# The sample rows' layer norm: mean from row sums of the weights, squares summed by ScalarE

## The chip, the cores and the metric

The kernel runs on one core of a Trainium2 chip. The metric is the device time of one execution in microseconds (us). Before the change it is 280.36 us, the median of three runs (280.11 to 280.70).

## The reference, cut to what matters

One inference step of a decoder with two layers and 1024 features, for 256 prompt rows and 8 sample rows. Layer 0 is a gated short convolution, layer 1 block-sparse attention. Each ends in a residual layer norm. The change sits in the last one, for the 8 sample rows:

```python
ys = (os_.reshape(Bs, Ts, D_MODEL) * jax.nn.silu(zs)) @ w_out_attn[j]
...
xs = _layernorm(DN_ALPHA * xs + ys, ln_g[i], ln_b[i])
...
def _layernorm(x, g, b):
    mu = x.mean(-1, keepdims=True)
    var = jnp.square(x - mu).mean(-1, keepdims=True)
    return (x - mu) * lax.rsqrt(var + LN_EPS) * g + b
```

## The kernel before, in words

Everything is written for one core in one fixed order; each engine runs its own list, and semaphores tie them. Weights come as slabs of 128x1024 floats, one a slot, over SyncE's queue (`load`, L112). ScalarE rounds a slab to its high part (`hi`, L124), VectorE subtracts for the low part (`lo`, L129), and TensorE multiplies high by high, high by low and low by high. Slots 0 to 31 are layer 0's input projection, 32 to 39 its output projection, 40 to 71 layer 1's input projection with attention between, 72 to 79 the slabs of layer 1's output projection. `begin(n)` issues what is hooked to slot n.

The end of the program, where the change lies, runs so:

- In slots 65 to 67 VectorE transposes x (features on partitions) into `kall` (`turn`, L884), and in slots 68 to 71 sixteen transfers on SyncE's queue, four a slot, move it back into `xf` as rows (`turn_move`, L889). Between them on the same queue stand the loads of the slabs 76 to 79, and behind them those of the gains `gb` and `g8`. The samples are taken out of `xf` beforehand by GpSimd (`sample_x`, L909) and turned by VectorE in slot 68 (`sample_turn`, L912). They lie in one tile `sx`, as 128 partitions of 128 features: the eight samples times eight feature groups, with every value twice in order to fill it. `xst` is x, `gs` the mixer's output (`sample_g`, L807), `so` the result.
- Prompt rows 0 to 127: TensorE forms their output projection `c0` in two banks over the eight slabs (`om`, L961). VectorE adds it to x (`evac`, L925), takes the statistics (`stats`, L928; `spread`, L931 and the Sqrt on ScalarE, L932), and the normalization is shared: columns 0 to 511 on VectorE (`one`, L939, and `two`, L944), 512 to 1023 on ScalarE and GpSimd (`other_way`, L951 to L953).
- Prompt rows 128 to 255 in three pieces of columns: 0 to 511 (in an `acc` bank), 512 to 767 (`c1b`), 768 to 1023 (`c1c`), 24 products each, with evacuation and statistics after each piece.
- The samples: 64 products `so` of the raw slabs with `gs` (L1062), each in two passes at full precision. While TensorE does them, VectorE normalizes rows 128 to 255.
- The samples' norm: VectorE adds x to `so` (L1073), takes statistics of each partition (L1074), spreads them over eight columns (L1076), a product with a 0/1 matrix from `g8` gathers the partitions of one sample (`st`, L1079), VectorE aggregates (L1083), ScalarE takes the root (L1084), and three VectorE operations (L1085 to L1087) finish. `ys_o` is stored (L1088).

Of the kernel before, what the change touches and what calls it, by code (L numbers as in the profile page):

```python
# [10 lines left out]
F32 = mybir.dt.float32  # L11
# [3 lines left out]
AF = mybir.ActivationFunctionType  # L15
ALU = mybir.AluOpType
AX = mybir.AxisListType

D = 1024
T = 256  # L20
B = 8
N = T + B
# [3 lines left out]
ALPHA = math.sqrt(2.0)  # L26
# [23 lines left out]
def build(tc, a):  # L50
    nc = tc.nc
    pe, act, dve, pool, sp = nc.tensor, nc.scalar, nc.vector, nc.gpsimd, nc.sync

    with ExitStack() as top:
# [4 lines left out]
        lnp = top.enter_context(tc.tile_pool(name="lnp", bufs=1))  # L59
        psp = top.enter_context(tc.tile_pool(name="psp", bufs=1, space=bass.MemoryType.PSUM))  # L60

        def acc_full():
            return psp.tile([128, 512], F32, tag="acc", bufs=3, name="acc")
# [4 lines left out]
        def att_tile(nm):  # L68
            return psp.tile([128, 512], F32, tag="att", bufs=3, name=nm)
# [20 lines left out]
        xf = cp.tile([128, NB, N], F32, name="xf")  # L90

        epst = cp.tile([128, 1], F32, name="epst")
# [5 lines left out]
        ident = cst[:, C_ID:C_ID + 128]  # L98
# [5 lines left out]
        raws, his, los = {}, {}, {}  # L104
# [41 lines left out]
        def run(n, phase):  # L146
            for f in hooks.pop((n, phase), []):
                f()
# [21 lines left out]
        def begin(n, end=True):  # L170
            for ph in ("dma", "pe", "s0", "hi", "lo", "s1a", "s1b", "s1", "s1c"):
                run(n, ph)
            if end:
                split_late(n)

        def split_late(n):
            run(n, "hi3")
            run(n, "lo3")
# [57 lines left out]
        onem = cp.tile([128, 2, 32], F32, name="onem")  # L236
# [161 lines left out]
        st = cst[:, C_ST:C_ST + 128].rearrange("p (r f b) -> p r f b", r=2, f=8)  # L398
# [129 lines left out]
        with tc.tile_pool(name="l1", bufs=1) as p1, ExitStack() as late_pool:  # L528
# [326 lines left out]
            for h in range(8):  # L855
                n = S + 16 + h
# [18 lines left out]

            turned = kall[:, 0:2048].rearrange("p (c m q) -> p c m q", c=8, m=8)
            xsb = xst = so = gs = g8 = None
            xt = xf.rearrange("p m n -> p (m n)")[:, 0:2048]

            def kv_tile(nm):  # L880
                return kvp.tile([128, 1024], F32, tag="kv", name=nm)
# [17 lines left out]
            def sample_room():  # L899
                nonlocal xsb, xst, so, gs, g8  # L900
                sx = kv_tile("sx")
                xsb, xst, so = (sx[:, 128 * i:128 * i + 128] for i in range(3))
                gs = sx[:, 512:1024].rearrange("p (c k r) -> p c k r", c=2, r=32)
                g8 = kv_tile("g8")[:, 0:392]
                pool.memset(sx, 0.0)

            def sample_x():
# [2 lines left out]

            def sample_turn():
                dve.transpose(xst, xsb)  # L912

            class Rows:

# [39 lines left out]
            def wide(d, k):  # L955
                return d[72 + k].rearrange("p a b -> p (a b)")

            def om(acc, k, c, c0, c1):
                t = np.s_[128 * c:128 * c + 128]
                for i, (m, d) in enumerate(((0, his), (1, his), (0, los))):  # L960
                    pe.matmul(acc, g[m][:, k, t], wide(d, k)[:, c0:c1],  # L961
                              start=k == 0 and i == 0, stop=k == 7 and i == 2)

            at(S + 26, "s1", sample_room)
            at(S + 26, "s1", sample_x)
            at(S + 28, "s1", sample_turn)
            for m in range(8):
                at(S + 25 + m // 3, "s1", turn, m)
# [15 lines left out]
            ps = ln.bcast_mm()  # L984
# [18 lines left out]
            for i in range(2, 32):  # L1003
                n = S + i
# [27 lines left out]
            ac = [ac[:, 512 * i:512 * i + 512] for i in range(2)]  # L1032
            for k in range(8):
                begin(72 + k)
                for h in range(2):
                    om(ac[h], k, 0, 512 * h, 512 * h + 512)
            r = rows[0]
# [7 lines left out]
            r.other_way(512, 1024)  # L1045
            r.two(0, 512)
            sp.dma_start(a["y_o"][0:128], r.x)

            r = rows[1]
            parts = [(0, 512), (512, 768), (768, 1024)]  # L1050
            last = [acc_full(), att_tile("c1b"), att_tile("c1c")]
            for i, (acc, (c0, c1)) in enumerate(zip(last, parts)):
                for k in range(8):
                    om(acc[:, 0:c1 - c0], k, 1, c0, c1)
                r.evac(c0, c1, acc[:, 0:c1 - c0])
                r.stats(i, c0, c1)

            ps = att_tile("so")[:, 0:128]
            for k in range(8):
                for c in range(2):  # L1060
                    for j in range(4):
                        pe.matmul(ps[32 * j:32 * j + 32], gs[:, c, k, :],  # L1062
                                  wide(raws, k)[:, 256 * j + 128 * c:256 * j + 128 * c + 128],
                                  start=k == 0 and c == 0, stop=k == 7 and c == 1)
            r.spread(3)
            r.one(0, 512)
            r.inverse()
# [1 line left out]
            r.two(0, 512)  # L1069
            sp.dma_start(a["y_o"][128:256, 0:512], r.x[:, 0:512])  # L1070
            r.one(512, 768)
            st = lnp.tile([128, 60], F32, name="row2")
            dve.scalar_tensor_tensor(so, xst, ALPHA, ps, ALU.mult, ALU.add)  # L1073
            dve.bn_stats(st[:, 0:6], so)  # L1074
            own8 = st[:, 12:60].rearrange("p (q e) -> p q e", e=6)
            dve.tensor_tensor(own8, g8[:, 384:392].rearrange("p (q o) -> p q o", o=1).to_broadcast([128, 8, 6]),  # L1076
                              st[:, 0:6].rearrange("p (o e) -> p o e", o=1).to_broadcast([128, 8, 6]), ALU.mult)
            t = att_tile("st")[:, 0:48]
            pe.matmul(t, g8[:, 256:384], st[:, 12:60], start=True, stop=True)  # L1079
            r.two(512, 768)  # L1080
            sp.dma_start(a["y_o"][128:256, 512:1024], r.x[:, 512:1024])

            dve.bn_aggr(st[:, 6:8], t)  # L1083
            act.activation(st[:, 8:9], st[:, 7:8], AF.Sqrt, bias=epst)  # L1084
            dve.scalar_tensor_tensor(so, so, st[:, 6:7], g8[:, 0:128], ALU.subtract, ALU.mult)  # L1085
            dve.reciprocal(st[:, 9:10], st[:, 8:9])
            dve.scalar_tensor_tensor(so, so, st[:, 9:10], g8[:, 128:256], ALU.mult, ALU.add)  # L1087
            sp.dma_start(a["ys_o"], so)  # L1088
# [75 lines left out]
```

## Time and profile before

| | before |
|---|---|
| median of three runs | 280.36 us |
| the profiled execution | 280.45 us |
| its span (first to last record) | 278.7 us |
| TensorE busy | 272.7 us, 98% |
| VectorE busy | 195.6 us, 70% |
| ScalarE busy | 155.3 us, 56% |
| mean granted TensorE clock | 0.996 |

Times in the trace are us from the span's start. A row of a timeline gives start, length, engine, line, operation, and output and input tiles; in square brackets stands how long the engine was idle before it and what ended that. PE is TensorE, DVE VectorE, ACT ScalarE, POOL GpSimd, SPq SyncE's queue. A matmul's shown length overlaps the next one's, so prices of products are taken from start to start.

### The profile page before, as it was taken

How to read it: one execution, taken by the hardware profiler on the slowest of the kernel's cores; microseconds unless marked ns; L12 is line 12 of the kernel's file. 1: busy time of each engine (PE TensorE's matmuls, PEld its weight loads, DVE VectorE, ACT ScalarE, POOL GpSimd, SP SyncE). 2: the span in 40 equal slices, each digit the busy share in tenths (PEclk: the TensorE clock that was granted, in tenths of full speed). 3: DMA queues.
4: the chain of work that ended last, by engine and by line, in shares of the span. 5: the costliest groups of instructions: out<-in, count | busy, mean ns of one | idle time of the engine just before them, and what ended most of it. 6: DMA issues, size and time to landing. Idle time of an engine off the chain costs nothing.

```text
span 278.7 us, 6245 instructions
## 1 busy us (share of the span) xinstructions
PE 272.7 (98%) x2330; PEld 255.6 (92%) x2330; DVE 195.6 (70%) x377; ACT 155.3 (56%) x294; POOL 59.8 (21%) x130
## 2 busy tenths in 40 slices
PE   8999999999999999999999999999999999999992
PEld 5999999999999999999998997999959987988891
DVE  3868976655766768969999498498626384993745
ACT  4876564444655538557776495567746752571101
POOL 2110532020101102850311158411100030000212
PEclk9999999999999999999999999999999999999998
DMA  7985989999666876134025999999864995781012
GB/s 230 410 266 189 310 274 331 385 373 356 230 211 224 295 238 221 43 119 152 2 75 194 387 399 348 359 335 304 277 223 149 311 379 173 236 290 61 0 78 85
DMA packets 24495, 66.34 MB, mean 238 GB/s; under 512 B 3090, under 2 KB 6930, under 8 KB 24466
## 3 DMA queue, kind: packets, MB, share of 16 engines
q1 hardware_dynamic: 24178, 65.63, 67.4%
q8 instruction: 18, 0.29, 0.4%
q10 hardware_dynamic: 288, 0.33, 0.4%
q14 instruction: 11, 0.09, 0.1%
HBM read 61.55 MB, written 3.35 MB: 233 GB/s over the span
## 4 chain that ended last, share of the span: by engine, by line
PE 98%; DVE 1%; issue 0%
PE acc L136 24%; PE acc L138 24%; PE acc L137 24%; PE c L961 4%; PE sd L716 3%; PE dps L768 3%; PE acc L961 2%; PE acc L465 2%; PE acc L466 2%; PE acc L469 1%; PE so L1062 1%; PE warmp L80 1%; PE s L649 1%; PE o L688 1%; PE c1b L961 1%; PE c1c L961 1%
## 5 line engine op out<-in xcount | busy, mean ns | idle before, releaser
L124 ACT CAST hi<-raw 128x1024 fp32r<-128x1024 f32 x76 | 79.2, 1049 | 35.2 <-DMA raw<-w 22.1
L129 DVE TENSOR_TENSOR lo<-raw,hi 128x1024 fp32r<-128x1024 f32 x76 | 92.7, 1230 | 7.6 <-ACT hi L124 7.4
L138 PE MATMUL acc<-m0h,lo 128*128 128x264 f32 (+1 forms) x280 | 79.4, 284 | 0.0
L137 PE MATMUL acc<-m0l,hi 128*128 128x264 f32 (+1 forms) x280 | 79.3, 283 | 0.0
L136 PE MATMUL acc<-m0h,hi 128*128 128x264 f32 (+1 forms) x280 | 79.3, 283 | 0.0
L136 PE MATMUL acc<-m1h,hi 128*128 128x264 f32 x264 | 76.6, 290 | 0.0
L138 PE MATMUL acc<-m1h,lo 128*128 128x264 f32 x264 | 74.8, 283 | 0.0
L137 PE MATMUL acc<-m1l,hi 128*128 128x264 f32 x264 | 74.7, 283 | 0.0
L136 PEld LDWEIGHTS acc<-m0h,hi 128*128 128x128 f32 x280 | 52.7, 188 | 0.2
L138 PEld LDWEIGHTS acc<-m0h,lo 128*128 128x128 f32 x280 | 52.8, 189 | 0.0
L137 PEld LDWEIGHTS acc<-m0l,hi 128*128 128x128 f32 x280 | 52.7, 188 | 0.0
L136 PEld LDWEIGHTS acc<-m1h,hi 128*128 128x128 f32 x264 | 49.7, 188 | 1.7 <-issue 1.7
L137 PEld LDWEIGHTS acc<-m1l,hi 128*128 128x128 f32 x264 | 49.7, 188 | 0.1
L138 PEld LDWEIGHTS acc<-m1h,lo 128*128 128x128 f32 x264 | 49.7, 188 | 0.0
L421 POOL COPY uo<-up 128x10 f32<-128x10 f32 x8 | 8.0, 1002 | 66.8 <-DVE up L420 58.9
L657 DVE TENSOR_TENSOR s<-s,cst 128x256 f32<-128x256 f32 x8 | 3.4, 430 | 14.7 <-PE s L649 14.7
L799 DVE TENSOR_TENSOR gt<-z,q 128x256 f32<-128x256 f32 x8 | 3.4, 423 | 9.4 <-ACT z L796 9.4
L932 ACT ACTIVATE row<-row,epst 128x1 f32<-128x1 f32 x2 | 0.6, 295 | 16.6 <-DVE row L931 16.6
L666 ACT ACTIVATE P<-s,mx 128x128 f32<-128x128 f32 (+1 forms) x16 | 6.6, 416 | 5.6 <-DVE mx L660 5.6
L796 ACT ACTIVATE z<-acc 128x264 f32<-128x264 f32 x8 | 3.1, 391 | 11.4 <-PE acc L138 11.4
L628 POOL COPY vs<-vh 128x8 f32<-128x8 f32 x8 | 1.6, 204 | 34.9 <-ACT vh L627 34.9
L466 PE MATMUL acc<-m0l,hi 128*128 128x264 f32 x32 | 8.9, 306 | 0.0
(215 smaller groups left out, 415.4 us busy)
## 6 DMA issues: line engine op xcount, KB each, us to landing
raw<-w SPq DMA_DIRECT2D x76, 512.0 KB, 4.7
kv<-kc SPq DMA_DIRECT2D x32, 256.0 KB, 5.7
kv<-vc SPq DMA_DIRECT2D x16, 512.0 KB, 6.6
first<-first SPq DMA_DIRECT2D x6, 388.0 KB, 6.9
k_o<-kall SPq DMA_DIRECT2D x8, 132.0 KB, 5.1
v_o<-vh SPq DMA_DIRECT2D x8, 132.0 KB, 5.2
xf<-kall SPq DMA_DIRECT2D x16, 64.0 KB, 3.1
kall<-gb SPq DMA_DIRECT2D x2, 512.0 KB, 5.0
```

The costliest lines, as they stand in the source:

```text
L124: act.copy(his[n][sl], raws[n][sl])
L129: dve.tensor_sub(los[n][sl], raws[n][sl], his[n].bitcast(F32)[sl])
L136: pe.matmul(acc, wh, mh[:, k, 0:w], start=first and k == ks[0], stop=False)
L137: pe.matmul(acc, wh, ml[:, k, 0:w], start=False, stop=False)
L138: pe.matmul(acc, wl, mh[:, k, 0:w], start=False, stop=last and k == ks[-1])
L421: pool.tensor_copy(uo[:, f], up[:, T:N + 2])
L465: pe.matmul(accs[s], wh, mh, start=k == 0, stop=False)
L466: pe.matmul(accs[s], wh, ml, start=False, stop=False)
L666: act.activation(P[sl], s_ps[h][sl], AF.Exp, bias=mx[:, 2 + i:3 + i], scale=SCALE, accum_out=mx[:, 4 + i:5 + i])
L716: pe.matmul(s[32 * j:32 * j + 16, 0:256], zq[:, o:o + 16], kt, start=step == 0 and i == 0, stop=step == 3 and i == 3)
L768: pe.matmul(dps[0][32 * j:32 * j + 32, 512 * c:512 * c + 512], pm[b2][pg][:, j, :], kv_tiles[step, j][:, 512 * c:512 * c + 512], start=ste ...
L961: pe.matmul(acc, g[m][:, k, t], wide(d, k)[:, c0:c1], start=k == 0 and i == 0, stop=k == 7 and i == 2)
```

## The change

- ScalarE forms the row sums of each raw slab 72 to 79 (`w_sum`, a copy into a scratch tile with a sum beside it): slabs 72 to 75 in the slots 76 to 79, slabs 76 to 79 behind the normalization of rows 0 to 127.
- VectorE sums x over the eight feature blocks (`sample_turn`), and behind the first piece of rows 128 to 255 it multiplies `gs` by the row sums, adds up, adds x, and copies the result to 128 columns (`sample_mean`).
- Between `c1b` and `c1c` TensorE sums `zrep` over the partitions with -1/1024: minus the mean of each sample, in an `acc` bank. VectorE copies it and forms `xst` = ALPHA x - mean.
- `so` begins with a product of the identity with `xst`, so that x and the mean are in the bank when it ends.
- Then ScalarE squares the bank with a sum beside it, VectorE multiplies the bank by the gain, `st` has one column (its 0/1 matrix is divided by 1024 on the host), and the root is taken of it. L1073 to L1076, L1083 and L1085 are gone.

```diff
             def sample_turn():
                 dve.transpose(xst, xsb)
+                dve.tensor_reduce(xsum, xf[:, :, T:N].rearrange("p m q -> p q m"), AX.X, ALU.add)
+
+            def w_sum(k):
+                act.activation(od, wide(raws, k), AF.Copy, accum_out=wsum[:, k:k + 1])
+
+            def sample_mean():
+                z = xsb.rearrange("p (k q) -> p k q", q=16)[:, :, 0:8]
+                w = wsum.rearrange("p (k o) -> p k o", o=1).to_broadcast([128, 8, 8])
+                dve.tensor_tensor(z, gs[:, 0, :, 0:32:4], w, ALU.mult)
+                dve.tensor_reduce(zsum, z.rearrange("p k q -> p q k"), AX.X, ALU.add)
+                dve.scalar_tensor_tensor(zsum, xsum, ALPHA, zsum, ALU.mult, ALU.add)
+                dve.tensor_copy(zrep.rearrange("p (j q e) -> p j q e", j=4, e=4),
+                                zsum.rearrange("p (o q e) -> p o q e", o=1, e=1).to_broadcast([128, 4, 8, 4]))
...
             for k in range(8):
                 begin(72 + k)
+                if k > 3:
+                    w_sum(k - 4)
...
             sp.dma_start(a["y_o"][0:128], r.x)
+            for k in range(4, 8):
+                w_sum(k)
...
                 for k in range(8):
                     om(acc[:, 0:c1 - c0], k, 1, c0, c1)
+                if i == 1:
+                    mean = acc_full()[:, 0:1]
+                    pe.matmul(mean, zrep, onem[:, 0, 0:1], start=True, stop=True)
                 r.evac(c0, c1, acc[:, 0:c1 - c0])
                 r.stats(i, c0, c1)
+                if i == 0:
+                    sample_mean()
+                if i == 1:
+                    dve.tensor_copy(st[:, 2:3], mean)
+                    dve.tensor_scalar(xst, xst, ALPHA, st[:, 2:3], ALU.mult, ALU.add)
 
             ps = att_tile("so")[:, 0:128]
+            pe.matmul(ps, ident, xst, start=True, stop=False)
...
             r.one(512, 768)
-            st = lnp.tile([128, 60], F32, name="row2")
-            dve.scalar_tensor_tensor(so, xst, ALPHA, ps, ALU.mult, ALU.add)
-            dve.bn_stats(st[:, 0:6], so)
-            own8 = st[:, 12:60].rearrange("p (q e) -> p q e", e=6)
-            dve.tensor_tensor(own8, g8[:, 384:392].rearrange("p (q o) -> p q o", o=1).to_broadcast([128, 8, 6]),
-                              st[:, 0:6].rearrange("p (o e) -> p o e", o=1).to_broadcast([128, 8, 6]), ALU.mult)
-            t = att_tile("st")[:, 0:48]
-            pe.matmul(t, g8[:, 256:384], st[:, 12:60], start=True, stop=True)
+            act.activation(xsb, ps, AF.Square, accum_out=st[:, 0:1])
+            dve.tensor_tensor(so, ps, g8[:, 0:128], ALU.mult)
+            t = att_tile("st")[:, 0:1]
+            pe.matmul(t, g8[:, 256:384], st[:, 0:1], start=True, stop=True)
             r.two(512, 768)
             sp.dma_start(a["y_o"][128:256, 512:1024], r.x[:, 512:1024])
-
-            dve.bn_aggr(st[:, 6:8], t)
-            act.activation(st[:, 8:9], st[:, 7:8], AF.Sqrt, bias=epst)
-            dve.scalar_tensor_tensor(so, so, st[:, 6:7], g8[:, 0:128], ALU.subtract, ALU.mult)
+            act.activation(st[:, 8:9], t, AF.Sqrt, bias=epst)
```

How the lists of the engines change shows in three places. First ScalarE at the end of the program, from the rounding of slab 78 to the last root (names with their numbers; `row0` and `row1` are the statistics of the two row blocks). Before:

```order
L124 CAST hi78_3659<-raw78_3549 128x1024
L124 CAST hi79_3661<-raw79_3596 128x1024
L932 ACTIVATE row0_3625<-row0_3625,epst_88 128x1
L951 ACTIVATE xf_87<-xf_87,row0_3625 128x512
L932 ACTIVATE row1_3626<-row1_3626,epst_88 128x1
L951 ACTIVATE xf_87<-xf_87,row1_3626 128x256
```

and now:

```order
L124 CAST hi79_3667<-raw79_3602 128x1024
L919 ACTIVATE zq_2035,wsum_1869<-raw72_3261 128x1024
L919 ACTIVATE zq_2035,wsum_1869<-raw73_3317 128x1024
L919 ACTIVATE zq_2035,wsum_1869<-raw74_3359 128x1024
L919 ACTIVATE zq_2035,wsum_1869<-raw75_3421 128x1024
L948 ACTIVATE row0_3631<-row0_3631,epst_88 128x1
L967 ACTIVATE xf_87<-xf_87,row0_3631 128x512
L919 ACTIVATE zq_2035,wsum_1869<-raw76_3465 128x1024
L919 ACTIVATE zq_2035,wsum_1869<-raw77_3511 128x1024
L919 ACTIVATE zq_2035,wsum_1869<-raw78_3555 128x1024
L919 ACTIVATE zq_2035,wsum_1869<-raw79_3602 128x1024
L948 ACTIVATE row1_3632<-row1_3632,epst_88 128x1
```

Four sums stand between the rounding of slab 79 and the root of rows 0 to 127, four behind the normalization of these rows (old L951, now L967).

Second, VectorE and TensorE at the middle piece of rows 128 to 255. VectorE before, from the first piece's evacuation to the third's:

```order
L925 SCALAR_TENSOR_TENSOR xf_87<-xf_87,acc_3717 128x512
L928 BN_STATS row1_3626<-xf_87 128x6
L925 SCALAR_TENSOR_TENSOR xf_87<-xf_87,c1b_3718 128x256
L928 BN_STATS row1_3626<-xf_87 128x6
L925 SCALAR_TENSOR_TENSOR xf_87<-xf_87,c1c_3719 128x256
```

and now, followed by TensorE's list at the change from `c1b` to `c1c`:

```order
L941 SCALAR_TENSOR_TENSOR xf_87<-xf_87,acc_3731 128x512
L944 BN_STATS row1_3632<-xf_87 128x6
L924 TENSOR_TENSOR sx_3361<-sx_3361,wsum_1869 128x8x8
L925 TENSOR_REDUCE zsum_1871<-sx_3361 128x8
L926 SCALAR_TENSOR_TENSOR zsum_1871<-xsum_1870,zsum_1871 128x8
L927 COPY zrep_1873<-zsum_1871 128x128
L941 SCALAR_TENSOR_TENSOR xf_87<-xf_87,c1b_3732 128x256
L944 BN_STATS row1_3632<-xf_87 128x6
L1083 COPY row2_1872<-acc_3788 128x1
L1084 TENSOR_SCALAR sx_3361<-sx_3361,row2_1872 128x128
L941 SCALAR_TENSOR_TENSOR xf_87<-xf_87,c1c_3733 128x256
```
```order
L977 MATMUL c1b_3732<-hi79_3667,m0h_89 128x256
L977 MATMUL c1b_3732<-hi79_3667,m0l_90 128x256
L977 MATMUL c1b_3732<-lo79_3677,m0h_89 128x256
L1077 MATMUL acc_3788<-onem_174,zrep_1873 128x1
L977 MATMUL c1c_3733<-hi72_3417,m0h_89 128x256
```

The mean's four operations stand ahead of the evacuation of `c1b`, the use of the mean behind it, and its product stands ahead of all products of `c1c`, which before followed `c1b` at once.

Third, SyncE's queue from the load of slab 76 to that of slab 77, with the semaphores that each waits for (those named DMAHW belong to earlier transfers). Before:

```order
L112 DMA raw76_3460<-w 128x1024 [waits DMAHW3_49,PE_49]
L889 DMA xf_87<-kall_1863 32x2x256 [waits DMAHW4_49,Pool_49]
L889 DMA xf_87<-kall_1863 32x2x256 [waits DMAHW5_49]
L889 DMA xf_87<-kall_1863 32x2x256 [waits DMAHW6_49]
L889 DMA xf_87<-kall_1863 32x2x256 [waits DMAHW7_49]
L112 DMA raw77_3505<-w 128x1024 [waits DMAHW0_49,PE_49]
```

and now:

```order
L112 DMA raw76_3465<-w 128x1024 [waits DMAHW3_49,PE_49]
L892 DMA xf_87<-kall_1863 32x2x256 [waits DMAHW4_49,DVE_49,Pool_49]
L892 DMA xf_87<-kall_1863 32x2x256 [waits DMAHW5_49]
L892 DMA xf_87<-kall_1863 32x2x256 [waits DMAHW6_49]
L892 DMA xf_87<-kall_1863 32x2x256 [waits DMAHW7_49]
L112 DMA raw77_3511<-w 128x1024 [waits DMAHW0_49,PE_49]
```

The order of the queue is the same, but the first of these moves waits for VectorE as well, namely for the new sum over `xf` (L916), which stands on VectorE right behind the sample's transposition (L912, now L915).

More of the change, by code (lines that the diff above doesn't have):

```diff
@@ L877, in build @@
             xsb = xst = so = gs = g8 = None
+            wsum, xsum, zsum = (lnp.tile([128, 8], F32, name=n) for n in ("wsum", "xsum", "zsum"))
+            st = lnp.tile([128, 10], F32, name="row2")
+            zrep = lnp.tile([128, 128], F32, name="zrep")
             xt = xf.rearrange("p m n -> p (m n)")[:, 0:2048]
@@ L903, in sample_room @@
                 gs = sx[:, 512:1024].rearrange("p (c k r) -> p c k r", c=2, r=32)
-                g8 = kv_tile("g8")[:, 0:392]
+                g8 = kv_tile("g8")[:, 0:384]
                 pool.memset(sx, 0.0)
@@ L1063, in build @@
                                   wide(raws, k)[:, 256 * j + 128 * c:256 * j + 128 * c + 128],
-                                  start=k == 0 and c == 0, stop=k == 7 and c == 1)
+                                  start=False, stop=k == 7 and c == 1)
             r.spread(3)
@@ L1126 @@
     g8 = np.concatenate([v[1][turned].reshape(8, 128)[own] for v in (lg, lb)]
-                        + [(same[:, None] == same) & (np.arange(128) % 4 < 2)[:, None],
-                           own[:, None] == np.arange(8)], 1).astype(f32)
+                        + [((same[:, None] == same) & (np.arange(128) % 4 < 2)[:, None]) / D], 1).astype(f32)
     stc = np.asarray(state_conv)[0]
```

## The prediction

> **What bounds the kernel now.** I read the page first, then the chain of work that ended last, then the timelines of the engines over the last 40 us. The page's busy times and the chain's shares by engine:
>
> ```profile
> PE 272.7 (98%) x2330; PEld 255.6 (92%) x2330; DVE 195.6 (70%) x377; ACT 155.3 (56%) x294; POOL 59.8 (21%) x130
> PE 98%; DVE 1%; issue 0%
> ```
>
> TensorE sets the end nearly everywhere: a wait of its own costs its full length, and whatever the others do beside it costs nothing. The one place where it doesn't is the last 3 us. The chain's last pieces (start, length, what; `c1c` is the last quarter of the prompt's second row block, `so` the sample's output product, `st` the group-statistics product):
>
> ```profile
> 266.57 2.83 PE c1c L961 x24
> 269.40 3.67 PE so L1062 x128
> ...
> 273.10 0.30 DVE sx L1073
> ...
> 274.21 0.43 PE st L1079 x2
> ...
> 275.43 0.15 DVE row L1086
> ...
> 275.61 0.35 DVE sx L1087
> ```
>
> From the end of `so` (269.40 + 3.67 = 273.07) to the last VectorE result (275.61 + 0.35 = 275.96) pass 2.89 us: the exposed tail, and all that the change can win. The profiled execution took 280.45 us (span 278.7, 1.75 around it), 0.09 over the median of the runs, 280.36. The sum is made against 280.45.
>
> **The tail, shortened.** The new tail is Square with its sum on ScalarE, `st` with one column, Sqrt, reciprocal, one scale-and-add. Rows for it: an activation with a sum over a 128x128 bank (timeline of ScalarE), and the old Sqrt:
>
> ```profile
> 215.44 0.37 ACT L666 ACTIVATE P<-s,mx 128x128 f32<-128x128 f32 x1 [0.36 <-DVE mx L660]
> 215.70 0.19 ACT L666 ACTIVATION_READ_ACCUMULATOR P<-s,mx 128x1 f32 x1
> 215.79 0.47 ACT L666 ACTIVATE P<-s,mx 128x256 f32<-128x256 f32 x1
> ...
> 275.08 0.29 ACT L1084 ACTIVATE row<-row,epst 128x1 f32<-128x1 f32 x1 [2.79 <-DVE row L1083]
> ```
>
> A sum costs a second instruction: it starts 0.26 us after the activation and runs 0.19, so Square ends at 0.45. Then `st` 0.40 (0.43 with 48 columns), Sqrt 0.29, reciprocal 0.15, scale-and-add 0.35, and five hand-overs of some 0.03: 1.79 us, so **-1.1 us** (-0.9 if Square is nearer 0.6; -1.3 if the sum is hidden and `st` takes 0.28). VectorE's product with the gain waits for Square, then `two` of row 1 follows (0.29 + 0.47 from +0.5 to +1.22), just ahead of the reciprocal at +1.26; were that cover gone it would cost about 0.1. Two stores now land closer together (size, median us from issue to landing):
>
> ```profile
> y_o<-xf SPq DMA_DIRECT2D x2, 256.0 KB, 2.0
> ys_o<-sx SPq DMA_DIRECT2D x1, 64.0 KB, 1.5
> ```
>
> The last piece of `y_o` is issued at about +1.3 and lands at +3.3; `ys_o`, issued at +1.82, would land at +3.3 too. They share the engines: **+0.1 us** (0 to 0.3).
>
> **What is laid ahead of it.** The shorter tail is bought with a mean that must be in the bank before `so`. Its path: eight row sums of the weights on ScalarE, four small operations on VectorE, one product on TensorE that stands between `c1b` and `c1c`. TensorE takes products in order, so this product's wait holds the whole of `c1c` and `so` back. When can it run? ScalarE's timeline, with the row-0 Sqrt and normalization between which and behind which the order puts the sums:
>
> ```profile
> 260.96 0.30 ACT L932 ACTIVATE row<-row,epst 128x1 f32<-128x1 f32 x1 [8.81 <-DVE row L931]
> 262.02 0.82 ACT L951 ACTIVATE xf<-xf,row 128x512 f32<-128x512 f32 x1 [0.76 <-DVE row L950]
> ```
>
> Sums 0 to 3 stand ahead of 260.96 where ScalarE idles 8.8 us: free. Sums 4 to 7 can't start before L951 lets go, 262.02 + 0.82 less the overlap of some 0.09 by which 215.79 follows 215.70: 262.75. One sum is a 128x1024 copy from SBUF with an accumulation; groups of ScalarE by shape, mean ns of one:
>
> ```profile
> L124 ACT CAST hi<-raw 128x1024 fp32r<-128x1024 f32 x76 | 79.2, 1049 | 35.2 <-DMA raw<-w 22.1 <-PE acc L137 12.1 <-DVE rp L606 1.1
> L816 ACT CAST m1h<-xf 128x264 fp32r<-128x264 f32 x8 | 3.3, 413 | 0.3
> L301 ACT ACTIVATE sqm<-xf 128x264 f32<-128x264 f32 x7 | 3.0, 425 | 6.1 <-DVE xf L280 5.2 <-POOL q L309 0.8
> L951 ACT ACTIVATE xf<-xf,row 128x256 f32<-128x256 f32 x1 | 0.6, 602 | 0.8 <-DVE row L950 0.8
> ```
>
> The cast takes 1.05; an activation with immediate scale is only 12 ns dearer than a cast at 264 columns, so 1.06. The accumulator read starts 0.1 before that ends and takes 0.19, and each sum waits for the one before (they share a scratch output), 0.03: 1.19 a sum. Bounds: 1.04 if the read adds only the 0.09 from 215.70 to 215.79 to the cast's 0.95 (1.05 less an overlap of 0.1); 1.48 if this activation costs like L951 with its two vector operands (602 at 256, 818 at 512, so 1250 at 1024). Sum 7 ends at 262.75 + 4 x 1.19 = 267.5 (266.9 to 268.7). Nearest VectorE rows for the four small operations, and VectorE's timeline at row 1:
>
> ```profile
> L778 DVE TENSOR_REDUCE zq<-zq 128x128 f32<-128x1024 f32 x1 | 2.0, 2035 | 0.0
> L213 DVE CAST hi<-first 128x128 fp32r<-128x128 f32 x1 | 0.2, 226 | 3.9 <-DMA first<-first 3.9
> L807 DVE TENSOR_TENSOR sx<-os__1868,zs 128x64 f32<-128x64 f32 x2 | 0.4, 266 | 0.0
> L950 DVE SCALAR_TENSOR_TENSOR row<-row 128x1 f32<-128x1 f32 x2 | 0.3, 158 | 0.1
> ```
> ```profile
> 264.50 0.69 DVE L928 BATCH_NORM_STATS2 row<-xf 128x6 f32<-128x512 f32 x1
> 266.61 0.42 DVE L925 SCALAR_TENSOR_TENSOR xf<-xf,c1b 128x256 f32<-128x256 f32 x1 [1.42 <-PE c1b L961]
> ```
>
> Product of 64 elements 0.27 (L807); strided reduce of 64 at L778's 2 ns each plus a start of 0.15, 0.27; scale-and-add 0.16; copy 0.23; four hand-overs 0.14: 1.07 us (0.85 to 1.3). VectorE is free from 265.2 and only waits for sum 7. `zrep` stands at 268.6. What queues behind on VectorE is row 1's `c1b` evacuation (from 266.61 to 268.6) with its statistics, the mean's copy and the sample's scaling, some 1.3 us: done by 270, before `c1c` is over, so hidden. TensorE's timeline, at the place itself and where the kernel does a like product (one column, full precision, two passes) and a 128x128 one:
>
> ```profile
> 266.29 0.28 PE L961 MATMUL c1b<-lo,m0h 128*128 128x256 f32 x1
> 266.41 0.28 PE L961 MATMUL c1c<-hi,m0h 128*128 128x256 f32 x1
> ```
> ```profile
> 184.93 0.28 PE L728 MATMUL sd<-onesf,pr 128*128 128x1 f32 x2
> 185.07 0.47 PE L648 MATMUL s<-kall,q 128*128 128x128 f32 x2
> ```
> ```profile
> 189.91 0.38 PE L648 MATMUL s<-kall,q 128*128 128x128 f32 x2
> 190.13 0.60 PE L649 MATMUL s<-kall,q 128*128 128x256 f32 x2
> ```
>
> The mean's product could start at 266.41 and starts at 268.6: TensorE stands still for **+2.2 us** (1.4 to 3.6). The product itself costs 0.14 in the stream (184.93 to 185.07); behind a wait one weight load of about 0.12 shows as well: **+0.25 us** (0.14 to 0.42, the whole `st`). The identity product ahead of `so` costs 0.22 from start to start (189.91 to 190.13): **+0.24 us** (0.2 to 0.3); its operand is ready by 270, `c1c` ends near 271.9.
>
> Does the clock hold through the stall? Granted clock (before DMA share and GB/s) in the tail, where TensorE's last work ends at 274.64:
>
> ```profile
> 276.40:276.50 0.10, 0.00 (x0) 0.00 (x0) 0.00 (x0) 0.00 (x0) 0.00 (x0) 0.67 0.00 0
> ```
>
> The clock falls 1.8 us after the last product of any kind. Read so, a stall of 2.2 us could do the same, and `c1c` and `so` behind it would run slow. But it also falls 3.4 us after the last dense stretch, which ended at 273.07 with only 0.43 us of work since; read so, 2.2 us are too short. I take the second reading, full clock and **0 us**, because the single product of 0.43 us in between is hardly work; the first is a rival. The Trainium skill, "TensorE: Matmul & The Clock Gate", section "What's actually happening", says that the gate closes after a window of about 3.4 us without work, and that these windows run free of the program. By that rule the trace's fall fits, and the gap alone would cost nothing.
>
> **The move on the queue.** The new sum of `x` (L916) reads `xf` where the row blocks are turned, so the fifth transfer of `xf` now waits for VectorE, and on SyncE all behind it: the three last weight slabs, the gains. SyncE's rows, VectorE's ahead of the new reduce, TensorE's first use of slab 79, and the landing of a slab (median of three here):
>
> ```profile
> 236.12 2.55 SPq L889 DMA_DIRECT2D xf<-kall  x4
> 238.76 0.54 SPq L112 DMA_DIRECT2D raw<-w  x1
> ...
> 245.13 0.53 SPq L112 DMA_DIRECT2D raw<-w  x1
> ```
> ```profile
> 240.53 0.31 DVE L912 STREAM_TRANSPOSE sx<-sx 128x128 f32<-128x128 f32 x1
> ```
> ```profile
> 256.62 0.39 PE L961 MATMUL c<-hi,m0h 128*128 128x512 f32 x1
> ```
> ```profile
> raw<-w SPq DMA_DIRECT2D x3, 512.0 KB, 3.9
> ```
>
> The reduce ends near 241.1, so the transfers move from 236.12 to 241.1 and slab 79 from 245.13 to 250.1. It lands at 254.0, its high part (1.05) is ready at 255.1, its low part (1.23) at 256.3; TensorE asks for them at 256.62 and 257.08. **0 us**, with 0.8 us to spare for the low part; a landing 1 us later would begin to cost. The sums 0 to 3 then run from 255.1 to 259.9, still ahead of 260.96. The reduce's own 0.25 on VectorE, the changed constant and the smaller `g8` cost nothing: TensorE waits for none of them there.
>
> **Sum:** 2.2 + 0.25 + 0.24 + 0.1 - 1.1 = +1.7 us, so 280.45 + 1.7 = 282.15, and 0.09 less against the median: **282.1 us**. With all bounds kind 1.4 + 0.14 + 0.2 + 0 - 1.3 = +0.4 (280.9); all unkind 3.6 + 0.42 + 0.3 + 0.3 - 0.9 = +3.7 (284.2).
>
> **The rivals.**
> - *Faster: TensorE finds the mean ready.* If the sums cost so little that `zrep` stands at 266.4, the stall is gone and the sum is 0.14 + 0.24 + 0.1 - 1.1 = -0.6: 279.8. That needs sum 7 at 265.3, (265.3 - 262.75) / 4 = 0.64 us a sum; even break-even (a stall of 0.6) needs 0.79. For it speaks that ScalarE is otherwise idle; against it, every 128x1024 row of ScalarE takes 1.05. Chance 0.05.
> - *The clock falls in the stall.* `c1c` then runs at half pace: +2.8 (its 2.83 again), 285.0. For: the clock row above. Against: its place 3.4 us behind `so`. Chance 0.07.
> - *Late slabs.* If slab 79 lands 1.5 to 2.5 us later than I put it, TensorE waits in row 0 as well; but row 0's Sqrt and with it sums 4 to 7 move along, so the stall adds: +0.5 to +1.5, 282.6 to 283.6. Chance 0.08.
> - *The tail doesn't shorten*, because the stores or VectorE's product end last: the 1.1 is lost, 283.2. For: the two landings at +3.3. Chance 0.05.
>
> The forecast keeps 0.75. About 0.2% (0.56 us) is what a measurement of this kernel can tell from no change; that much slower is 280.9. Only the kindest end of the forecast falls within it: same 0.07, faster 0.05, slower 0.88. The range of 281.0 to 283.7 leaves out the clock's fall, the faster case and the kindest end.
>
> **What would show it.** In the changed profile: a wait of TensorE of about 2.2 us on VectorE's `zrep` between `c1b` and `c1c`, the largest of the program; sums 4 to 7 on ScalarE 1.19 apart from 262.75; `c1c`, `so` later by 2.5; from `so`'s end to the last VectorE result 1.8 instead of 2.9; the fifth `xf` transfer near 241; granted clock 1.0 until `so` is done. The forecast is wrong if TensorE passes the mean's product without that wait, if the sums are closer than 0.8, or if TensorE waits for a slab around 256.

## The result and the profile after

The changed kernel takes 283.19 us (median of six runs, 281.79 to 284.06) against 280.24 us before (six runs, 279.91 to 280.77): the ratio is 1.0101, 95% interval 1.0073 to 1.013. It is slower by 1%, or 2.95 us. Its runs spread more than twice as wide as the old kernel's (2.3 us against 0.9), and the profiled one is the shortest of the six: 281.79 us, span 280.0, mean granted clock 1.000, where the other five show 0.992 to 0.994. A run's mean clock alone does not tell a slow stretch: runs of the old kernel show 0.994 to 1.000 as well, since a fall behind the last product counts in it and costs nothing (in the profile before the clock falls to 0.50 at 276.43, which makes the 0.996). This profile therefore shows the change at full clock; what the other runs add needs a second profile, below.

From the page after, busy times and the chain's shares by engine:

```profile
PE 272.6 (97%) x2334; PEld 255.1 (91%) x2334; DVE 195.7 (70%) x380; ACT 165.1 (59%) x312; POOL 60.7 (22%) x130
PE 92%; ACT 2%; DMA 2%; DVE 2%; issue 0%; SPq 0%; DVEq 0%
```

TensorE has as much work as before, but the chain that ended last now leaves it: ScalarE, busy 10 us more, stands on it. The chain's last pieces after (start, length, what; L919 is one row sum, L924 to L927 the mean's four operations, L1077 the mean's product, L1087 the identity product):

```profile
266.04 1.16 ACT zq L919 x2
...
267.22 0.28 DVE sx L924
...
268.01 0.24 DVE zrep L927
...
268.29 0.38 PE acc L1077 x2
268.68 2.94 PE c1c L977 x24
271.62 0.22 PE so L1087 x2
271.84 3.68 PE so L1091 x128
...
275.54 0.38 ACT sx L1101 x2
...
275.96 0.40 PE st L1104 x2
...
276.87 0.35 DVE sx L1109
```

The chain runs from the last row sum through VectorE's four operations into the mean's product, and only from there along TensorE. The list of waits after names the gap (total us, times, longest):

```profile
PE acc L1077 <- DVE zrep L927: 2.0, 1, 2.0
```

Behind `so` the gain is there too: from 271.84 + 3.68 = 275.52 to 276.87 + 0.35 = 277.22 pass 1.70 us instead of 2.89. ScalarE's timeline shows what sets the wait, the first of the four late sums and the start of the next (the second instruction reads the sum out):

```profile
262.50 1.05 ACT L919 ACTIVATE zq<-raw 128x1024 f32<-128x1024 f32 x1
263.45 0.19 ACT L919 ACTIVATION_READ_ACCUMULATOR zq<-raw 128x1 f32 x1
263.67 1.06 ACT L919 ACTIVATE zq<-raw 128x1024 f32<-128x1024 f32 x1
```

From start to start the four late sums take 1.18 us each (262.50 to 267.22 where VectorE starts behind the last). And the slabs: SyncE's delayed moves, its load of slab 79, ScalarE's and VectorE's rounding of that slab, and TensorE's first use of its low part:

```profile
240.82 2.51 SPq L892 DMA_DIRECT2D xf<-kall  x4
...
249.79 0.53 SPq L112 DMA_DIRECT2D raw<-w  x1
```
```profile
254.16 1.05 ACT L124 CAST hi<-raw 128x1024 fp32r<-128x1024 f32 x1 [2.45 <-DMA raw<-w]
```
```profile
255.24 1.23 DVE L129 TENSOR_TENSOR lo<-raw,hi 128x1024 fp32r<-128x1024 f32 x1 [2.28 <-ACT hi L124]
```
```profile
256.83 0.40 PE L977 MATMUL c<-lo,m0h 128*128 128x512 f32 x1
```

The low part is ready at 256.47, and TensorE takes it at 256.83: the cover is down to 0.36 us, but it holds.

### The profile page after: what moved, and what is told of

Read it like the earlier page. It is cut to its first block, busy times and chain, and to the rows that moved or that the text cites. A ratio compares the mean times of both kernels' runs of the same rounds, so it can differ in the third digit from the quotient of the medians.

```text
span 280.0 us, 6276 instructions
## 1 busy us (share of the span) xinstructions
PE 272.6 (97%) x2334; PEld 255.1 (91%) x2334; DVE 195.7 (70%) x380; ACT 165.1 (59%) x312; POOL 60.7 (22%) x130
## 4 chain that ended last, share of the span: by engine, by line
PE 92%; ACT 2%; DMA 2%; DVE 2%; issue 0%; SPq 0%; DVEq 0%
PE acc L136 24%; PE acc L138 24%; PE acc L137 23%; PE c L977 4%; PE sd L716 3%; PE dps L768 3%; DMA first<-first 2%; ACT zq L919 2%; PE so L1091 1%; PE s L649 1%; PE o L688 1%; PE acc L465 1%; PE c1c L977 1%; PE acc L466 1%; PE acc L469 1%; PE pt L679 1%
## 5 line engine op out<-in xcount | busy, mean ns | idle before, releaser
L421 POOL COPY uo<-up 128x10 f32<-128x10 f32 x8 | 9.0, 1122 | 65.4 <-DVE up L420 59.3
L429 DVE SCALAR_TENSOR_TENSOR t<-up,cst,t 128x256 f32<-128x256 f32 x8 | 3.9, 483 | 9.6 <-ACT t L428 9.6
L465 PE MATMUL acc<-m0h,hi 128*128 128x264 f32 x32 | 8.3, 290 | 0.4 <-ACT m0h L209 0.2
```

Source lines behind the costliest of these rows:

```text
L421: pool.tensor_copy(uo[:, f], up[:, T:N + 2])
L465: pe.matmul(accs[s], wh, mh, start=k == 0, stop=False)
```

## The experiments

Two theories stood against each other for the 1.4 us by which the median lies above the profiled run. Theory A: TensorE's clock falls because of the wait. Theory B: slab 79 lands late in most runs. The first four kernels ran on one chip beside 17 runs of the kernel before (median 279.95), the last four on another chip beside 29 runs (280.22).

**1. The changed kernel again**, without an edit.

> The changed kernel once more, unedited, for a second profile and more times. Its first six runs spread from 281.79 to 284.06 us (before: 279.91 to 280.77), and only the fastest, the profiled one, kept the clock at 1.00; the others show 0.992 to 0.994. Theory A (the wait for the mean costs 2.4 us at full clock, and in most runs the clock falls behind it): median near 283.2, and the profile shows either a clock of 1.00 and about 281.8, or a stretch at half clock in c1c or so and 283 or more. Theory B (the spread comes from slab 79 landing late): a slow profile shows TensorE waiting near 256 us, with the clock at 1.00 until so is done.

Measured: 283.59 us (281.21 to 284.05), ratio 1.0105 (1.0075 to 1.0135). The profile caught a long run, 283.88 us. Its chain at the same place:

```profile
268.88 0.38 PE acc L1077 x2
269.26 4.46 PE c1c L977 x24
273.72 0.22 PE so L1087 x2
```

`c1c` takes 4.46 us instead of 2.94. Its windows (length; busy us and instructions of PE, PEld, DVE, ACT, POOL; then the granted clock, DMA share, GB/s):

```profile
267.00:268.00 1.00, 0.00 (x0) 0.00 (x0) 0.20 (x1) 0.77 (x2) 0.00 (x0) 1.00 0.99 406
268.00:269.00 1.00, 0.12 (x1) 0.13 (x2) 0.90 (x5) 0.00 (x0) 0.00 (x0) 1.00 0.16 62
269.00:270.00 1.00, 1.00 (x6) 1.00 (x7) 0.93 (x4) 0.00 (x0) 0.00 (x0) 0.62 0.00 0
270.00:271.00 1.00, 1.00 (x7) 1.00 (x6) 0.00 (x0) 0.00 (x0) 0.00 (x0) 0.50 0.00 0
...
272.00:273.00 1.00, 1.00 (x8) 1.00 (x8) 0.00 (x0) 0.00 (x0) 0.00 (x0) 0.67 0.00 0
273.00:274.00 1.00, 1.00 (x13) 0.88 (x15) 0.24 (x1) 0.00 (x0) 0.00 (x0) 1.00 0.00 0
```

TensorE is idle through 267 to 268; the clock is still whole then. It halves at 269.25 (0.62 in that window is 0.25 at full and 0.75 at half), when TensorE is at work again, and is back at 272.66 (0.67 in its window): 3.4 us later. Its products show both paces from start to start:

```profile
266.64 0.28 PE L977 MATMUL c1b<-lo,m0h 128*128 128x256 f32 x1
268.88 0.38 PE L1077 MATMUL acc<-onem,zrep 128*128 128x1 f32 x2 [1.96 <-DVE zrep L927]
...
269.59 0.41 PE L977 MATMUL c1c<-lo,m0h 128*128 128x256 f32 x1
269.80 0.41 PE L977 MATMUL c1c<-hi,m0h 128*128 128x256 f32 x1
...
272.85 0.28 PE L977 MATMUL c1c<-hi,m0h 128*128 128x256 f32 x1
272.97 0.28 PE L977 MATMUL c1c<-hi,m0l 128*128 128x256 f32 x1
```

0.21 us a product in the slow stretch, 0.12 behind it. No wait of TensorE stands near 256 in this profile either. This is theory A's picture. Of the 2.1 us between this run and the first profiled one (283.88 and 281.79), the slow stretch is 1.5; the other 0.6 had come up before the wait (`c1b` ends at 266.92, there at 266.33), no more than runs of the old kernel differ by.

**2. The sum of x early**, so that the transfers and slabs 77 to 79 go out as before:

```diff
 def sample_x():
     for c in range(2):
         pool.tensor_copy(..., xf[:, 4 * c:4 * c + 4, T:N])
+    dve.tensor_reduce(xsum, xf[:, :, T:N].rearrange("p m q -> p q m"), AX.X, ALU.add)
...
     dve.transpose(xst, xsb)
-    dve.tensor_reduce(xsum, xf[:, :, T:N].rearrange("p m q -> p q m"), AX.X, ALU.add)
```

> The sum of x over the feature blocks is taken two slots earlier, before the row blocks are moved, so the transfers and slabs 77 to 79 no longer wait for VectorE. Theory A: the late slabs cost nothing; the time stays at 283.2 (within 0.4) with the same spread; SyncE's fifth xf transfer back near 236, slab 79 issued near 245. Theory B: the slabs are the extra; the time falls to about 281.8 in all runs.

Measured: 282.94 us (281.30 to 283.69), ratio 1.0103 (1.008 to 1.0126). SyncE's queue is back at its old times:

```profile
235.51 2.53 SPq L892 DMA_DIRECT2D xf<-kall  x4
...
244.51 0.54 SPq L112 DMA_DIRECT2D raw<-w  x1
```

The spread is unchanged, from 281.3 to 283.7, with clocks of 0.990 to 0.994 in the three longest runs. So the late slabs aren't the cause. Three of six runs are long here against ten of the twelve of the unedited kernel; whether that is chance the runs can't tell.

**3. TensorE kept at work through the wait:**

```diff
-                    mean = acc_full()[:, 0:1]
+                    mean = acc_full()
+                    for _ in range(9):
+                        pe.matmul(mean, one[:, 0:128], one, start=True, stop=True)
+                    mean = mean[:, 0:1]
                     pe.matmul(mean, zrep, onem[:, 0, 0:1], start=True, stop=True)
```

> Nine products of ones (128x512, bf16) stand ahead of the mean's product and are overwritten by it, so that TensorE works through most of the 2 us wait; they take about 9 x 0.22 = 1.9 us. The wait itself stays. Theory A: the clock no longer falls, all runs come near the fast one, 281.8, with a clock of 0.995 or more and a spread as before the change. Theory B: unchanged, 283.2.

Measured: 281.91 us (281.42 to 282.75), ratio 1.0064 (1.0046 to 1.0082); every clock 0.996 or more. Its chain (L1078 are the added products, L1080 the mean's):

```profile
266.80 1.91 PE acc L1078 x8
...
268.73 0.38 PE acc L1080 x2
269.11 2.95 PE c1c L977 x24
```

The mean comes no earlier and nothing useful is computed in between, yet the median falls by 1.7 us against the unedited kernel on the same chip, to about where the forecast at full clock had put it (279.95 + 1.7 = 281.65). The records show eight of the nine products. That shows theory A: the rest of the loss is the clock, let go by the idle stretch.

**4. The new tail alone**, without row sums, mean and its product (`w_sum`, `sample_mean`, the sum of x at L916 and L1077 left out, `xst` only scaled by ALPHA; the lines that change rather than go):

```diff
-                    dve.tensor_copy(st[:, 2:3], mean)
-                    dve.tensor_scalar(xst, xst, ALPHA, st[:, 2:3], ALU.mult, ALU.add)
+                    dve.tensor_scalar(xst, xst, ALPHA, None, ALU.mult)
```

> Only the new tail: the row sums, the mean and its product are left out, xst is ALPHA x without the mean (so the mean is not subtracted from the samples). The identity product and the new tail stay. Forecast's terms: -1.1 for the tail, +0.24 identity, +0.1 stores: 280.24 - 0.8 = 279.5. If the tail doesn't shorten (stores or VectorE's product end last): 280.5 or more.

Measured: 279.46 us (278.92 to 280.52), ratio 0.9982 (0.997 to 0.9994). From its chain, the identity product, Square and the last operation:

```profile
269.48 0.22 PE so L1076 x2
...
273.40 0.38 ACT sx L1090 x2
...
274.73 0.35 DVE sx L1098
```

From Square's start to the last result pass 1.68 us (273.40 to 274.73 + 0.35), as in the changed kernel (275.54 to 277.22); the identity product costs 0.22. The gain is there, but in the times it is 0.5 us, not the expected 0.8; the interval reaches from 0.2 to 0.8 and does not rule that out.

**5. The mean's product behind `c1c`**, the identity product at the end of `so` (on top of edit 2):

```diff
-                if i == 1:
+                if i == 2:
                     mean = acc_full()[:, 0:1]
                     pe.matmul(mean, zrep, onem[:, 0, 0:1], start=True, stop=True)
...
-                if i == 1:
-                    dve.tensor_copy(st[:, 2:3], mean)
-                    dve.tensor_scalar(xst, xst, ALPHA, st[:, 2:3], ALU.mult, ALU.add)
...
-            pe.matmul(ps, ident, xst, start=True, stop=False)
...
-                                  start=False, stop=k == 7 and c == 1)
+                                  start=k == 0 and c == 0, stop=False)
...
             r.other_way(768, 1024)
+            dve.tensor_copy(st[:, 2:3], mean)
+            dve.tensor_scalar(xst, xst, ALPHA, st[:, 2:3], ALU.mult, ALU.add)
+            pe.matmul(ps, ident, xst, start=False, stop=True)
```

> The sum of x is taken early as in e1; the mean's product moves behind c1c, and the identity product, which needs the mean, from the head of so to its end. Nothing else changes, all the same sums are formed. If the loss is the wait between c1b and c1c and the clock that falls behind it, both are gone: as e4 (279.5) plus the mean's product, 0.14 to 0.25, so 279.6, clock 0.995 or more, slightly faster than before. If the sums themselves, or VectorE's wait for them, cost something: 280.5 or more.

Measured: 279.56 us (278.92 to 280.68), ratio 0.9972 (0.9957 to 0.9987). Its chain (L1077 the mean, L1087 `so`, L1096 the identity):

```profile
269.04 0.11 PE acc L1077 x2
269.15 3.63 PE so L1087 x128
272.79 0.43 PE so L1096 x2
...
273.24 0.38 ACT sx L1100 x2
```

All eight sums and the mean are formed as in the change, and nothing waits for them: TensorE passes the mean's product in 0.11 us. This version beats both kernels, the old one by 0.3%.

**6. to 8. The wait made shorter and longer**, by how many of the eight sums stand ahead of row block 0's root on ScalarE (all on top of edit 2; the mean's product stays between `c1b` and `c1c`). Six ahead:

```diff
-                if k > 3:
-                    w_sum(k - 4)
+                for j in {4: (0, 1), 5: (2, 3), 6: (4,), 7: (5,)}.get(k, ()):
+                    w_sum(j)
...
-            for k in range(4, 8):
+            for k in range(6, 8):
                 w_sum(k)
```

and in the same way five and three.

> The sum of x early as in e1; six of the eight sums stand ahead of row block 0's root on ScalarE and two behind. The mean's product stays between c1b and c1c. Sum 7 ends 2 x 1.18 = 2.4 earlier, about 264.4, zrep stands at 265.5, and TensorE reaches the product at 266.2: no wait. By the forecast's terms 0.14 + 0.24 + 0.1 - 1.2 = -0.7 against before, near 279.5; the clock holds.

> As e6 with five sums ahead and three behind: a wait of about 0.8 us for the mean. If the clock falls only when most of a window of 3.4 us is idle, it holds here in every run: e6 plus 0.8 to 0.9, so 280.4. If any wait lets it fall: spread up to 282 as in e1.

> As e6 with three sums ahead and five behind: a wait of about 3.2 us. Full clock would give e1's fast runs (281.3 to 282.3) plus 1.2, near 283. If windows of 3.4 us run free and one with some 1.5 us idle closes the gate (13 of 18 runs with a wait of 2.0 were long), every run here loses the clock for one window: 284.4 to 285, with a small spread and every clock at 0.994 or less.

| sums ahead and behind | wait for the mean | median, us | over the kernel before on its chip | range, us | ratio (interval) |
|---|---|---|---|---|---|
| 6 and 2 | none listed | 279.87 | -0.35 | 279.14 to 280.81 | 0.9987 (0.9971 to 1.0002) |
| 5 and 3 | 0.8 | 280.55 | +0.33 | 280.03 to 281.13 | 1.0008 (0.9996 to 1.002) |
| 4 and 4 (edit 2) | 2.0 | 282.94 | +2.99 | 281.30 to 283.69 | 1.0103 (1.008 to 1.0126) |
| 3 and 5 | 3.1 | 284.96 | +4.74 | 282.50 to 286.63 | 1.0155 (1.0113 to 1.0197) |

The waits are those of TensorE in the lists of waits, here that of five and three, and that of three and five:

```profile
PE acc L1077 <- DVE zrep L927: 0.8, 1, 0.8
```
```profile
PE acc L1077 <- DVE zrep L927: 3.1, 1, 3.1
```

Six and two was expected at 0.7 under the kernel before and came at 0.35, with an interval from 0.8 under it to level. Its trace shows where the rest went: `zrep` stood at 266.29, not 265.5, so TensorE's product started 0.28 us behind the last one of `c1b` instead of 0.12, and it cost 0.38 and 0.11 more in `c1c`, where 0.14 had been put. From there to five and three the time grows by 0.7, about as the wait does, and all twelve clocks are 0.997 or more. From 0.8 to 2.0 it grows by 2.7 (each against the kernel before on its own chip), twice as much as the wait, and the spread opens. With 3.1 the profile shows the clock gone for longer; its chain and two windows:

```profile
270.00 5.30 PE c1c L977 x24
```
```profile
268.20:268.40 0.20, 0.00 (x0) 0.00 (x0) 0.06 (x1) 0.11 (x2) 0.00 (x0) 0.80 0.00 0
...
269.00:270.00 1.00, 0.58 (x3) 0.58 (x3) 0.93 (x4) 0.00 (x0) 0.00 (x0) 0.50 0.00 0
```

The clock falls at 268.32, while TensorE still waits (the mean's product starts at 269.42), and is back at 275.15; nearly all of `c1c` runs at half clock, 5.30 us. The expectation of this run failed: not every run lost the clock, the times spread over 4.1 us, and in the profile it was gone for 6.8 us and not for 3.4. By their clocks four of the six lost it (0.985 to 0.991); two show 1.000, one of them short (282.50), the other long (284.46), and why that one is long without a fall in its clock stays open.

## Why the prediction was right in the direction and wrong in one step

The forecast was 282.1 us in a range of 281.0 to 283.7; measured are 283.19. The kernel is slower for the reason given, TensorE's wait at the mean's product. Step by step:

- **The sums on ScalarE.** 1.19 us each from 262.75 were expected, 1.18 from 262.50 came. The activation is priced like the cast, and the accumulator read and the wait on the one before each add what the rows said. (The unkind bound of 1.48 does not come out of its rows: 1.25 with the same additions of 0.13 is 1.38. With it the wait's upper bound of 3.6 would be 3.2; the forecast itself doesn't change.)
- **VectorE's four operations:** 1.03 us (267.22 to 268.25) for 1.07.
- **The wait:** 2.0 us for 2.2. In this execution the whole of the end runs 0.24 us earlier; ScalarE moves with it.
- **The mean's product** costs 0.39 and leaves `c1c` 0.11 longer, 0.5 for 0.25; **the identity** 0.22 for 0.24. The three together, from the end of `c1b` (266.05 + 0.28 = 266.33) to that of `so`: 9.19 us against 6.50 before (266.57 to 273.07), +2.69, which is the forecast's 2.2 + 0.25 + 0.24. That the sum fits so well is in part luck: the wait was 0.2 shorter and the product 0.25 dearer than forecast.
- **The tail:** -1.2 for -1.1. **The stores:** from the last result to the end of the span 2.78 us for 2.74 before, next to nothing for 0.1.
- **The slabs on SyncE's queue:** moved as forecast (240.82 for 241.1; slab 79 at 249.79 for 250.1), and no wait followed; the cover was 0.36 us, not 0.8, since from its issue to ScalarE's start on the slab passed 4.4 us (249.79 to 254.16) instead of 3.9.
- **The clock: the step that failed.** It was put at "full clock and 0 us", with the reading that it falls only after 3.4 us without dense work, and its fall was left to a rival with a chance of 0.07. In 10 of the 12 runs of the changed kernel the time lies 1 to 3 us above the two short ones, and in the profile of such a run the clock is halved for 3.4 us within `c1c`, which costs 1.52 (4.46 for 2.94). That is the rival's mechanism; its price of 2.8 was too high, since the clock came back before `c1c` was done, and since a product at half clock takes 0.21 us for 0.12: even in the run with three and five `c1c` costs no more than 2.4 extra (5.30 for 2.94).

So the forecast describes the shortest runs (281.21 and 281.79 us, where 281.9 was expected, 1.7 over that result's 280.24), and the median lies 1.3 above. That it still lies in the range is luck: by its own words the range left the clock's fall out, and its upper end was laid out for a longer wait.

The mistake lay in how the tail's single row of clock was read. The fall there at 276.43 fitted both a short gap and a long one, and the choice went to the long one on the argument that a product of 0.43 us is hardly work. The second profile shows that far more work doesn't help: taking 3.41 us, the time from fall to return, as the length of time whose work decides, the stretch ahead of the fall (265.83 to 269.24) held 1.09 us of `c1b` and 0.37 behind the wait, 1.46 us in all, and the clock fell. The Trainium skill, "TensorE: Matmul & The Clock Gate", section "What's actually happening", has windows of about 3.4 us that run free of the program and says that one idle window closes the gate (what halves the clock). The length and the free running agree with these runs: a fall that lasts 3.4 us, the same kernel now with it and now without, and in the run with three and five a fall at 268.32, a return at 275.15 and a fall at 281.97, each 6.83 or twice 3.41 from the one before. That the window must be idle doesn't agree: one that was 43% busy closed it. The prediction's sentence that the old kernel's fall fits that rule holds only if the 0.43 us of work in the 3.41 us ahead of it count as none.

The kept traces also narrow down where the limit lies. Counted from each trace's own clock changes in steps of 3.41 us, the stretches behind which the clock fell were at most 49% busy (46% and 49% at the end of the runs of experiment 5 and of six and two), and every stretch that was 53% busy or more, ahead of it at full clock, kept the clock. By this the short runs kept the clock because of where the same wait of 2.0 us lay against these stretches: in the first profile of the changed kernel the stretch with most of the wait was 58% busy, in that of edit 2 it was 53%. So about half of the stretch is the limit here, inferred from ten traces; a wait of 0.8 us, 23% of 3.41, stays clear of it, and one of 2.0, 58%, passes it or not by where it falls. A wait of 3.1 us would spare the clock only when it lies almost evenly across two stretches, so two such runs of six with a clock of 1.000 are more than this lets expect; no trace of them was kept, and they stay unexplained.

## What to carry to other kernels

A product that needs a late value belongs behind the work that doesn't need it: on an engine that takes its list in order, the place of an instruction is a wait for all that follows, and moving the mean's product and the one that needs it here turned a loss of 1% into a gain of 0.3%. Price a long wait of TensorE not at its length only: at 0.8 us it cost about what it was long, at 2.0 us in most runs three quarters as much again (1.52 us in the profiled one); between the two nothing was measured. Where the wait can't be moved, products that nobody needs can hold the clock, as the nine here did, which took 1.7 us off the median.

## What the runs showed of the hardware

- A wait of TensorE of 2.0 us lets its clock fall in most executions of the same program and not in others: of 18 runs with that wait (changed kernel and edit 2), 13 lie at 282.86 us or more, 5 between 281.21 and 282.33. The 36 runs with a wait of 0.8 us or none (experiment 5, six and two, five and three) spread as the old kernel's own on that chip (1.1 to 1.8 us within a kernel, against 1.6), with clocks of 0.995 or more.
- The fall need not come while TensorE waits: in the second profile of the changed kernel TensorE was at work from 268.88, and the clock halved at 269.25, to return 3.4 us later. With the wait of 3.1 us it fell in the wait, at 268.32.
- At full clock, 3.41 us that were at most 49% busy were followed by the fall and 3.41 us that were 53% busy or more were not, in all ten traces. Coming back took more: with three and five the first 3.41 us behind the fall were 68% busy (2.31 us), and the clock stayed at half for as long again.
- A sum beside an activation on ScalarE is an instruction of its own: 0.19 us, of which 0.1 overlaps the activation; with the wait for the one before, 128x1024 elements take 1.18 us from start to start. One cast of that size takes 1.05, and two that follow each other at once 1.98 (profile before, 250.17).
